# A two-layer hybrid decoder step on one core: sink as a score column, first roots in banks, other names for four banks

## The chip, the core and the metric

The kernel runs on one core of one Trainium2 chip. Time is device microseconds (us) from the start of the program to its end. Before the change the median of three runs is 2172.99 us. The engines are called PE (matrix products), ACT (elementwise functions), DVE and POOL (elementwise arithmetic) and SP (issues the large loads). PE writes to eight PSUM banks; ACT and DVE read and write them too.

## The reference, cut to what matters

Two layers, each with an FFN (feed-forward), a mixer (attention beside a gated recurrence) and a second FFN, on 512 prompt positions and 8 sequences of 8 sample positions, width 1024. Between the stages stands a root-mean-square norm with a modulation taken from a vector c.

```python
mod = (jax.nn.silu(c) @ w_ada + b_ada)
sh1, sc1, g1, sh2, sc2, g2, sh3, sc3, g3 = jnp.split(mod, N_MOD, axis=-1)
x = x + FFN_RES * g1 * swiglu(modulate(x, sh1, sc1), w1_gate, w1_up, w1_down)
h = modulate(x, sh2, sc2)              # rms_norm(x) * (1 + sc) + sh
q, k, v, xr, gr = jnp.split(h @ w_in, SPLITS, axis=-1)
...
s = s - slopes * dist
s = jnp.where(valid[:, None, None], s, NEG_INF)
sink = jnp.broadcast_to(sinks..., s.shape[:-1] + (1,))
p = jax.nn.softmax(jnp.concatenate([s, sink], axis=-1), axis=-1)[..., :-1]
...
x = x + g2 * (merged @ w_out)
x = x + FFN_RES * g3 * swiglu(modulate(x, sh3, sc3), w2_gate, w2_up, w2_down)
```

The softmax has one more column than there are keys, the learned sink of the head; its weight enters the sum and nothing else.

## The kernel before

Activations lie transposed: 1024 features as 8 blocks of 128 partitions, 576 positions in two halves of 288 columns, h=0 (64 sample positions and 224 of the prompt) and h=1. Float32 operands are split into a high and a low part: ACT writes the high part (`split` L218, a cast at L219), DVE or POOL the low part (L220). A product of one weight block with one half is three matmuls 128x288: high by high, high by low, low by high. The order on PE is the order in which the program writes matmuls and transposes (`pin` ties each to the one before); on the other engines it is set by a scheduler that follows the same program.

**The start.** `first_norm` (L383) makes the first roots: five diagonal matrices, and 12 small matmuls by ones that spread the roots over all partitions, into the tp and nrm banks; ACT copies them to SBUF (L402, `reps`). `ada_first` (L339) makes the modulation in four quarters q: 64 small matmuls of cT with weights that come by DMA into the pv bank, a copy on DVE (L349), one transpose (L209 into tp), and the bias (L354, L359). Quarter 0 stands on PE before the norm's 12 matmuls. `opened` then modulates feature blocks 2q and 2q+1 of both halves (`modulate` L544: DVE L560, L565 for the sample columns, DVE L569, ACT L580 for the high part, DVE L581 for the low part). In the first weight pair the six products of `jobs` go round by round: round q adds feature blocks 2q and 2q+1, so it needs quarter q. `E2` says before which product of a round the next quarter's matmuls and, at the second number, its transpose stand. `jobs` runs j, then h, then wi (0 gate, 1 up): the first two products of a round read h=0, the next two h=1. Of the eight weight splits of the pair, POOL makes six and DVE two.

**Openings.** Where a stage follows another, `opening` (L270) starts the next stage's first four products while the last feature block of x is still being added up. `pend` is the norm of x; `pend.add` puts a square (ACT, L131) into a bank named by `self.rest` and adds it to `acc` on DVE (L132). `PEND` and the line after the first product say at which product this stands, and with that which of the mm banks, taken in turn, the scratch gets. There are five openings (L206, `ps_mm<-hn,t`). After them `act` (L640) makes the silu of the pair; `self.modded` holds it behind the last high part of `modulate`.

**Attention.** `sample_chain` (4 a layer, one softmax each) and `prompt_chain` (8 a layer, two each) write scores into an sc bank. `soft` (L1258): DVE adds the distance term, takes the row maximum with the sink (L1263) and subtracts the sink from it (L1265); ACT takes the exponentials and their sum (L1267) and that of the sink (L1268); DVE adds (L1269), inverts (L1270) and, with ACT, scales P (L1275, L1273). PE then transposes P into tp. `keys` and `queries` (L992, L996) transpose the tokens of one block into tp, from where ACT and DVE scale them into SBUF (L1008, L1010). While these chains run, PE also has the products of the mixer (`ps_mm`), woven in by hand. Norms inside the mixer go through `tick` (L1222): `reduce` of one norm, `finish` LAG ticks later, then the next. The later ada blocks (`ada_steps`, L478) end with a DVE copy (L496) that the transposes at L500 wait for.

## Time and profile before

| | us |
|---|---|
| median of three runs | 2172.99 (2168.06 to 2173.04) |
| the profiled execution | 2171.54 |
| its span | 2169.7 |
| PE busy / DVE busy / ACT busy / POOL busy | 2099.1 / 1556.5 / 1014.7 / 778.7 |

A row of a timeline has: start in us, duration in us, engine, source line, operation, output<-inputs, shapes, count, and in brackets the engine's idle time before it with what ended that. Successive rows of an engine overlap a little, since instructions are pipelined; the step is the difference of the starts. A row of the list of waits has the engine and line that waited, what it waited for, and then: us in total, times, longest. A row of the table of windows has, for each stretch, its length, the busy time and the instruction count of each engine, the granted PE clock as a share of full speed, DMA share and GB/s. L1263 is a line of the code above.

### The profile page before, as it was taken

To read this page: it belongs to the slowest core of one execution; us is meant where nothing else is said; L and a number is where in the kernel's file an instruction comes from. 1 tells how busy PE (TensorE), PEld (TensorE's weight loads), DVE (VectorE), ACT (ScalarE), POOL (GpSimd) and SP (SyncE) were. 2 spreads that over 40 slices of the span, in tenths; PEclk is the share of its full clock that TensorE was granted. 3 is DMA by queue.
4 is the path that set the end of the run, shared out by engine and by line. 5 is a ranking of instruction groups with operands and counts; after the bars stand their busy time and mean duration, and the time that the engine had idled before them with its cause. 6 is when DMAs were issued, how large, how long until landed. Compare 5 with 4: busy or idle time off the path is not lost.

```text
span 2169.7 us, 40424 instructions
## 1 busy us (share of the span) xinstructions
PE 2099.1 (97%) x15856; PEld 1978.3 (91%) x15856; DVE 1556.5 (72%) x3701; ACT 1014.7 (47%) x2305; POOL 778.7 (36%) x671
## 2 busy tenths in 40 slices
PE   6999999999999999999999999999999999999999
PEld 6889789999879888889999999999997899999998
DVE  5766677675787876576678866776677789677665
ACT  4333434366575433333354543344566664334432
POOL 2142323344427432233245333232552474323430
PEclk8999999999999999999999999999999999999999
DMA  8844633331212265464341322232313022223221
GB/s 293 279 146 171 225 114 114 98 117 45 72 49 80 88 223 196 174 214 136 117 159 56 111 80 83 89 107 78 98 44 79 23 77 95 82 91 104 81 75 45
DMA packets 162364, 250.11 MB, mean 115 GB/s; under 512 B 7275, under 2 KB 125435, under 8 KB 154974
## 3 DMA queue, kind: packets, MB, share of 16 engines
q1 hardware_dynamic: 162018, 247.46, 34.7%
q8 instruction: 124, 2.03, 0.4%
q14 instruction: 66, 0.54, 0.1%
q10 hardware_dynamic: 156, 0.07, 0.0%
HBM read 244.62 MB, written 4.87 MB: 115 GB/s over the span
## 4 chain that ended last, share of the span: by engine, by line
PE 66%; DVE 8%; ACT 4%; issue 3%; POOL 1%; DMA 0%; ACTq 0%; POOLq 0%
PE ps_mm L843 19%; PE ps_mm L206 12%; PE ps_mm L918 8%; PE ps_sc L918 8%; PE ps_sc L843 7%; PE ps_sc L206 6%; DVE u L896 2%; ACT wh L219 2%; PE ps_pv L491 1%; PE ps_pv L206 1%; DVE wl L220 1%; ACT t L219 1%; DVE u L220 1%; PE ps_tp L209 1%; PE ps_nrm L206 1%
## 5 line engine op out<-in xcount | busy, mean ns | idle before, releaser
L849 POOL TENSOR_TENSOR P<-raw 128x512 f32<-128x512 f32 x156 | 233.1, 1507 | 724.5 <-DVE wl L220 421.4
L219 ACT CAST wh<-raw 128x512 fp32r<-128x512 f32 x498 | 298.6, 619 | 343.6 <-PE ps_mm L843 103.6
L220 DVE TENSOR_TENSOR wl<-raw,wh 128x512 fp32r<-128x512 f32 x408 | 328.6, 818 | 58.2 <-ACT wh L219 45.3
L219 ACT CAST wh<-P 128x512 fp32r<-128x512 f32 x312 | 188.0, 618 | 285.7 <-PE ps_sc L918 185.4
L220 DVE TENSOR_TENSOR wl<-P,wh 128x512 fp32r<-128x512 f32 x312 | 249.4, 814 | 83.6 <-ACT wh L219 75.2
L843 PE MATMUL ps_mm<-hn,wh 128*128 128x288 f32 x1248 | 255.6, 296 | 0.3 <-ACT t L882 0.3
L843 PE MATMUL ps_sc<-hn,wh 128*128 128x288 f32 x1248 | 254.9, 296 | 0.0
L843 PE MATMUL ps_mm<-u,wh 128*128 128x288 f32 x936 | 222.7, 299 | 5.1 <-ACT t L878 3.3
L843 PE MATMUL ps_mm<-t,wh 128*128 128x288 f32 x936 | 221.2, 297 | 0.7 <-DVE t L855 0.6
L843 PEld LDWEIGHTS ps_mm<-hn,wh 128*128 128x128 f32 x1248 | 199.8, 188 | 11.1 <-issue 6.7
L843 PEld LDWEIGHTS ps_sc<-hn,wh 128*128 128x128 f32 x1248 | 200.2, 188 | 9.2 <-issue 9.2
L843 PE MATMUL ps_mm<-hn,wl 128*128 128x288 f32 x624 | 184.0, 295 | 1.4 <-DVE wl L220 1.4
L843 PE MATMUL ps_mm<-u,wl 128*128 128x288 f32 x624 | 184.4, 296 | 0.0
L843 PE MATMUL ps_sc<-hn,wl 128*128 128x288 f32 x624 | 184.0, 295 | 0.0
L918 PE MATMUL ps_sc<-t,wh 128*128 128x288 f32 x608 | 180.7, 297 | 2.6 <-DVE ps_sc L648 1.8
L918 PE MATMUL ps_mm<-t,wh 128*128 128x288 f32 x608 | 179.5, 300 | 3.5 <-ACT t L219 2.8
L918 PE MATMUL ps_mm<-u,wh 128*128 128x288 f32 x608 | 179.8, 297 | 2.6 <-DVE u L220 2.6
L918 PE MATMUL ps_sc<-u,wh 128*128 128x288 f32 x608 | 179.9, 296 | 0.9 <-DVE u L220 0.9
L918 PE MATMUL ps_mm<-t,wl 128*128 128x288 f32 x608 | 178.9, 296 | 0.9 <-DVE wl L220 0.9
L918 PE MATMUL ps_sc<-t,wl 128*128 128x288 f32 x608 | 179.4, 295 | 0.0
L843 PEld LDWEIGHTS ps_mm<-u,wh 128*128 128x128 f32 x936 | 158.3, 188 | 18.0 <-ACT t L878 7.7
L843 PEld LDWEIGHTS ps_mm<-t,wh 128*128 128x128 f32 x936 | 158.8, 188 | 11.7 <-issue 5.4
(412 smaller groups left out, 5412.7 us busy)
## 6 DMA issues: line engine op xcount, KB each, us to landing
raw<-in_w_ada_dram SPq DMA_DIRECT2D x60, 1024.0 KB
raw<-in_w_gate_dram SPq DMA_DIRECT2D x44, 1024.0 KB
raw<-in_w_up_dram SPq DMA_DIRECT2D x44, 1024.0 KB
raw<-in_w_down_dram SPq DMA_DIRECT2D x44, 1024.0 KB
raw<-in_w_in_dram SPq DMA_DIRECT2D x14, 1024.0 KB
raw<-in_w_ada_dram SPq DMA_DIRECT2D x16, 512.0 KB
raw<-in_w_out_dram SPq DMA_DIRECT2D x4, 1024.0 KB
raw<-in_w_out_dram SPq DMA_DIRECT2D x8, 512.0 KB
```

The lines of the kernel that those rows point to most:

```text
L206: return self.pin(self.nc.tensor.matmul(*a, **k))
L209: return self.pin(self.nc.tensor.transpose(*a, **k))
L219: a = self.nc.scalar.copy(hi, src)
L220: b = (self.nc.gpsimd if pool else self.nc.vector).tensor_tensor(lo, src, hi.bitcast(F32), ALU.subtract)
L491: nc.tensor.matmul(acc[32 * j:32 * j + 32, :n], self.cT[:, k, :], raw[:, j * n:(j + 1) * n], start=(k == 0), stop=(k == KT - 1), tile_posi ...
L843: nc.tensor.matmul(ps[:, :HALF], a[x][:, k, :], b[k][y], start=start and k + n == 0, stop=k == 3 and n == 2, skip_group_check=True)
L849: nc.gpsimd.tensor_tensor(t, s[x] if x == 1 else x, s[y] if y == 2 else y, op)
L896: nc.vector.tensor_tensor(c, c, gate[i][:, hs], ALU.mult)
L918: mm(ps[:, :HALF], u[x][:, f, :], hid[f][y][:, hs], start=f + n == 0, stop=f == nf - 1 and n == 2)
```

## The change

- **Sink as a column.** P gets a column for the sink, filled by an ACT copy ahead of the scores; the exponential with its sum runs over it, and the subtraction (L1265), the sink's own exponential (L1268) and the addition (L1269) go. Each of the 40 calls of `soft` loses two small DVE instructions and one of ACT; 40 ACT copies come.
- **First roots kept in banks, gate products first.** The norm's matmuls stand ahead of quarter 0 on PE, in tp and pv, and `modulate` reads the roots there; the two ACT copies go. POOL makes all eight splits. `jobs` runs wi, j, h. `E2` is (3,4) in rounds 0 to 2.
- **Opening scratch** is named behind the second product instead of the first.
- **Silu** of the openings is held behind feature block 3 alone.
- **Queries** of blocks 3 and 4 go to the pv bank instead of tp.
- **Tick** waits one more tick between a `finish` and the next `reduce`.
- **ada_steps**' copy goes from DVE to ACT.

```diff
-E1, E2, E3 = True, ((2, 4), (0, 2), (0, 1), ()), 6
+E2 = ((3, 4), (3, 4), (3, 4), ())
...
-                if pend and h == 0 and (b, k) == (0, 0):
+                if pend and h == 0 and (b, k) == (1, 0):
                     self.rest(pend.add(KT - 1, self.done.pop((KT - 1, 1))))
...
-            acc = self.ps("pv")
+            acc = self.start[1][:, HALF:]
...
-            tp = self.ps("tp")
+            tp = self.start[0][:, HALF:]
...
-        reps = [self.ps(tag) for tag in ("tp", "nrm")]
+        reps = self.start = [self.ps(tag) for tag in ("tp", "pv")]
...
-            nc.vector.tensor_copy(ev[:, :n], acc[:, :n])
+            nc.scalar.copy(ev[:, :n], acc[:, :n])
...
+            if k == 3:
+                self.modded = r
...
-                    jobs = [(j, h, wi) for j in range(2) for h in range(2) for wi in range(2)]
+                    jobs = [(j, h, wi) for wi in range(2) for j in range(2) for h in range(2)]
...
-            tp = self.ps("tp")
+            tp = self.ps("tp" if t < 3 else "pv")
...
-        elif self.queue and self.queue[0][1] <= self.now:
+        elif self.now > self.idle and self.queue and self.queue[0][1] <= self.now:
...
-        nc.vector.tensor_tensor(es, nm, sinks, ALU.subtract)
         for i, p in enumerate(pts):
             nc.scalar.activation(p, p, AF.Exp, bias=nm[:, i:i + 1], scale=-1.0, accum_out=dn[:, i:i + 1])
-        nc.scalar.activation(es, es, AF.Exp)
-        nc.vector.tensor_tensor(dn, dn, es, ALU.add)
...
+        for kv in range(NKV):
+            nc.scalar.copy(pt[kv][:, :, nk * W], self.skp[:, l, gp, 2 * kv:2 * kv + 2])
```

PE at the start, before the change, from the transpose of quarter 1 on (each product is six such rows, of which one stands; hn is the modulated x, wh and wl weights, pT the copied quarter):

```order
L209 MATMUL ps_tp_420<-ident,pT_406 128x128 [waits DVE_49]
L206 MATMUL ps_mm_337<-hn_301,wh_315 128x288
...
L206 MATMUL ps_nrm_338<-hn_301,wh_327 128x288
...
L206 MATMUL ps_pv_458<-t_205,cT 32x128 [waits DMAHW4_49,PE_49]
...
L206 MATMUL ps_mm_333<-hn_301,wh_309 128x288 [waits Activation_49]
...
L206 MATMUL ps_sc_334<-hn_301,wh_321 128x288
```

And with the change:

```order
L207 MATMUL ps_nrm_330<-hn_295,wh_309 128x288
...
L210 MATMUL ps_tp_225<-ident,pT_405 128x128 [waits DVE_49]
L207 MATMUL ps_sc_331<-hn_295,wh_315 128x288
...
L207 MATMUL ps_mm_332<-hn_295,wh_315 128x288
...
L207 MATMUL ps_mm_327<-hn_295,wh_303 128x288 [waits Activation_49]
...
L207 MATMUL ps_mm_328<-hn_295,wh_303 128x288 [waits Activation_49]
```

Between the transpose and the next round's first product there are now two products, and no ada matmuls (ps_pv); the second product of a round reads h=1 where it read h=0.

DVE in the first sample chains of layer 0, before, after the root steps (L533 to L535) of a keys block; the P, sm and ps_sc are those of `soft`:

```order
L1008 TENSOR_SCALAR u_6309<-ps_tp_6484,qg 128x128 [waits Activation_49]
...
L1130 TENSOR_TENSOR u_6287<-u_6287,ps_mm_6417 128x512 [waits DVE_49]
L1269 TENSOR_TENSOR sm_6502<-sm_6502,sm_6501 128x1 [waits Activation_49]
L1263 ISA P_6546,sm_6547<-ps_sc_6540,nds,sks,sel 128x192 [waits PE_49]
...
L1270 RECIPROCAL sm_6502<-sm_6502 128x1 [waits DVE_49]
L1265 TENSOR_TENSOR sm_6548<-sm_6547,sks 128x1 [waits DVE_49]
L1275 TENSOR_SCALAR P_6499<-P_6499,sm_6502 128x192 [waits DVE_49]
```

And with the change:

```order
L1268 RECIPROCAL sm_6490<-sm_6490 128x1 [waits Activation_49]
L532 SCALAR_TENSOR_TENSOR ps_mm_6405<-tiny_6438,ps_mm_6405 128x8 [waits DVE_49]
L1273 TENSOR_SCALAR P_6487<-P_6487,sm_6490 128x192 [waits DVE_49]
L1129 TENSOR_TENSOR u_6275<-u_6275,ps_mm_6405 128x512 [waits DVE_49]
L1007 TENSOR_SCALAR u_6297<-ps_tp_6472,qg 128x128 [waits Activation_49]
L1264 ISA P_6531,sm_6533<-ps_sc_6525,nds,sks,sel 128x192 [waits PE_49]
...
L1268 RECIPROCAL sm_6534<-sm_6534 128x1 [waits Activation_49]
L1273 TENSOR_SCALAR P_6531<-P_6531,sm_6534 128x192 [waits DVE_49]
```

The inversion and the scaling of the first P now stand ahead of L1129 (L1130 before), and so does their wait for ACT's exponential; the second query copy of the block (L1007, L1008 before) has moved from ahead of these rows to behind them.

PE at the queries of block 3 in layer 0, before:

```order
L206 MATMUL ps_mm_7109<-hn_5430,wl_6681 128x288
L209 MATMUL ps_tp_7153<-ident,u_6379 128x128 [waits PE_49]
L209 MATMUL ps_tp_7153<-ident,u_6379 128x128 x3
L206 MATMUL ps_sc_7162<-u_6305,u_6308 128x256 [waits DVE_49]
...
L209 MATMUL ps_tp_7209<-ident,P_7045 128x128 [waits DVE_49]
```

And with the change:

```order
L207 MATMUL ps_mm_7067<-hn_5418,wl_6660 128x288
L210 MATMUL ps_pv_7111<-ident,u_6367 128x128 [waits PE_49,Activation_49]
L210 MATMUL ps_pv_7111<-ident,u_6367 128x128 x3
L207 MATMUL ps_sc_7120<-u_6293,u_6296 128x256 [waits DVE_49]
...
L210 MATMUL ps_tp_7161<-ident,P_7009 128x128 [waits DVE_49]
```

The transposes go to pv and wait for ACT as well; the transposes of P that follow are the same.

## Rows read from the trace of the kernel before

**Rows 1.** The page's busy times (us, share of the span, instructions)

```profile
PE 2099.1 (97%) x15856; PEld 1978.3 (91%) x15856; DVE 1556.5 (72%) x3701; ACT 1014.7 (47%) x2305; POOL 778.7 (36%) x671
```

**Rows 2.** The list of waits, engine PE, whole span

```profile
PE ps_mm L206 <- DVE acc L132: 6.9, 5, 1.4
PE ps_pv L206 <- DMA raw<-in_w_ada_dram: 6.4, 2, 4.0
PE ps_mm L206 <- ACT hn L580: 5.2, 1, 5.2
PE ps_tp L209 <- DVE P L1275: 4.4, 2, 2.2
PE ps_tp L209 <- DVE u L1008: 3.5, 2, 1.8
PE ps_tp L500 <- DVE pT L496: 2.3, 1, 2.3
PE ps_nrm L206 <- DVE ps_mm L593: 2.1, 2, 1.1
PE ps_sc L206 <- DVE ps_sc L648: 1.6, 3, 0.5
```

**Rows 3.** Timeline of the start, PE and DVE

```profile
24.08 1.78 PE L206 MATMUL ps_tp<-diag,ones 64*128 64x64 f32 x6
26.99 0.42 PE L209 MATMUL ps_tp<-ident,pT 128*128 128x128 f32 x1
28.10 0.69 DVE L220 TENSOR_TENSOR wl<-raw,wh 128x512 fp32r<-128x512 f32 x1
28.91 1.75 DVE L220 TENSOR_TENSOR wl<-raw,wh 128x512 fp32r<-128x512 f32 x1
32.60 0.61 PE L206 MATMUL ps_mm<-hn,wh 128*128 128x288 f32 x1 [5.18 <-ACT hn L580]
```

**Rows 4.** Table of windows, a stretch of the start and one after a wait

```profile
34.00:36.00 2.00, 2.00 (x9) 1.82 (x8) 1.37 (x4) 0.56 (x2) 0.00 (x0) 0.50 1.09 348
36.00:38.00 2.00, 2.00 (x66) 1.71 (x65) 0.00 (x0) 0.00 (x0) 0.00 (x0) 0.99 1.09 349
941.00:944.00 3.00, 3.00 (x15) 3.00 (x14) 1.55 (x5) 0.27 (x1) 0.00 (x0) 0.50 0.62 180
```

**Rows 5.** Timeline of the second round, PE and DVE

```profile
39.68 0.27 PE L209 MATMUL ps_tp<-ident,pT 128*128 128x128 f32 x1
43.35 0.53 PE L206 MATMUL ps_mm<-hn,wh 128*128 128x288 f32 x2
44.26 0.51 DVE L581 SCALAR_TENSOR_TENSOR hn<-nt,mod,hn 128x288 fp32r<-128x288 f32 x1
```

**Rows 6.** Timeline of two openings, PE and POOL

```profile
697.06 1.46 POOL L578 TENSOR_TENSOR hn<-nt,hn 128x224 fp32r<-128x224 f32 x2
1550.33 1.86 PE L206 MATMUL ps_mm<-hn,t 128*128 128x288 f32 x12 [1.35 <-DVE acc L132]
1550.76 0.67 POOL L578 TENSOR_TENSOR hn<-nt,hn 128x224 fp32r<-128x224 f32 x1
```

**Rows 7.** Timeline, ACT at the later ada copy

```profile
937.80 0.61 ACT L219 CAST wh<-raw 128x512 fp32r<-128x512 f32 x1
```

**Rows 8.** Timeline of a sample chain, PE, POOL and DVE

```profile
1626.78 0.33 PE L209 MATMUL ps_tp<-ident,u 128*128 128x128 f32 x1
1628.90 2.49 POOL L220 TENSOR_TENSOR wl<-raw,wh 128x512 fp32r<-128x512 f32 x2 [2.52 <-ACT wh L219]
1629.02 1.17 DVE L1265 TENSOR_TENSOR sm<-sm,sks 128x1 f32<-128x1 f32 x1
1630.11 1.40 DVE L1275 TENSOR_SCALAR P<-P,sm 128x192 f32<-128x192 f32 x1
1631.65 0.41 PE L209 MATMUL ps_tp<-ident,P 128*128 128x128 f32 x2 [2.20 <-DVE P L1275]
```

**Rows 9.** Timeline, ACT at the queries of block 3

```profile
1670.47 0.50 ACT L1273 ACTIVATE P<-P,sm 128x256 f32<-128x256 f32 x1
```

More of the change, by code (lines that the diff above doesn't have):

```diff
@@ L53 @@
 SLOT = 608
+SINK = 2 * 128 + 1
 STEPS = (1, 4)
@@ L164, in __init__ @@
         self.done = {}
-        self.now, self.cur, self.queue, self.ended = 0, None, [], []
+        self.now, self.idle, self.cur, self.queue, self.ended = 0, -1, None, [], []
     BUFS = {"t": 14, "u": 12, "P": 4, "pT": 3, "raw": 4, "wh": 4, "wl": 4, "hn": 4, "sq": 2, "acc": 2, "nt": 3, "mod": 2,
@@ L398, in first_norm @@
                             start=True, stop=True)
-        self.reps = []
-        for ps in reps:
-            self.reps.append(self.t("sq", [P, HALF]))
-            nc.scalar.copy(self.reps[-1], ps[:, :HALF])
     def params(self):
@@ L1449, in run @@
         first = self.ada_first(0, loads)
-        if E1:
-            next(first)
         self.first_norm()
-        if not E1:
-            next(first)
+        next(first)
         next(first)
@@ L1460, in opened @@
                 for h in range(2):
-                    self.modulate(hn, h, self.mods[0], 0, self.reps[h], 2, range(2 * q, 2 * q + 2))
+                    self.modulate(hn, h, self.mods[0], 0, self.start[h], 2, range(2 * q, 2 * q + 2))
                 yield q
```

45 lines of the change are left out of this document (24 added, 21 removed).

## The prediction

> **What bounds the kernel now.** I read the busy times first: PE is busy for 2099.1 of 2169.7 us [rows 1], so only about 70 us of the span are PE waiting, and the change leaves PE the same matmuls and transposes. Other engines matter only where PE waits for them. The second view is therefore the list of PE's waits, in which the reader is to look for the lines that the change touches [rows 2]: the openings' accumulation (L132, five waits, 6.9 us), the first modulated block (L580, 5.2), P of the softmax (L1275, 4.4 in two), the query copies (L1008, 3.5 in two), the ada copy (L496, 2.3), a norm's reduce (L593, 2.1 in two) and the silu's product (L648, 1.6 in three). Together 26.0 us; no edit can give more than that by waits alone. The third view are the timelines around each, to see what is late next. The table of windows adds the PE clock: at 34 to 36 us it is at half (1.2 of 2.4 GHz), 9 matmuls in 2.00 us; from 36 on it is full; at 941 to 944, behind the wait for the ada copy, it is at half once more [rows 4]. So a wait can cost more than its length: 3.0 us at half give back about 1.5.
>
> The sum is made against the profiled execution's own 2171.54 us (1.84 around the span). The median of the three runs is 1.45 above it, inside their spread.
>
> **Start.** PE idles 5.18 us ahead of the first product at 32.60 [rows 3]. Two things leave that path. The norm's 12 matmuls and the transpose behind them run from 24.08 on; the transpose comes at 26.99 [rows 3]. Ahead of quarter 0 they would run inside a wait for DMA of which PE has 6.4 us [rows 2], so the transpose moves up by up to 2.9 us. The two weight splits on DVE, 0.69 and 1.75 [rows 3], go to POOL: up to 2.3 by their steps (the second ends in a step of 1.67). The ACT copies of the roots were beside this. At most that is 5.2. Against it, POOL now makes four splits of the second weight beside the modulation, where it made two, and a DVE instruction beside POOL can be late by about one split: 1.75 against 0.69 is such a case. I take 4.5, with 3.3 to 5.8 as bounds.
>
> The new order takes some of it back. From the transpose at 39.68 to the end of the last low part of h=1 (44.26 and 0.51) are 5.1 us [rows 5]. Before, the next round's first product came 3.67 us behind the transpose, at 43.35 [rows 5], with the ada matmuls in between, and h=1 was needed only by the third product; no wait shows. Now two products stand between, and the second product of the round reads h=1. Twelve matmuls run in 1.86 us with the tail of the last one, 1.6 by their step [rows 6]. So PE has 1.6 us for the two products, 0.8 for the round's first and about 0.7 of the second: 3.1 of the 5.1. It waits 2.0 in each of three rounds: 6.0 us in all, 4.5 to 6.6 as bounds, by how early DVE is.
>
> The clock rose some 3.5 us after products began [rows 3, 4]. If it rises as late after an earlier start, nothing changes; if it rises at 36 as now, 4.5 us more run at half and 2.3 are lost. I take 1.0, with 0 and 4.0 (2.3, and one fall to half as at 941) as bounds. Start in all: 4.5 - 6.0 - 1.0 = 2.5 us lost, bounds 7.3 lost and 1.3 gained.
>
> **Openings.** The second product waited for a bank that Square and the addition of block 6 still read. It gets the free bank; the scratch, which is needed later, takes the late one. Next late are the low parts that POOL makes: in the mixer's opening one ends at 1551.43 (1550.76 and 0.67), while PE began again at 1550.33; in the second FFN's two end at about 697.8 [rows 6], where PE waited until 698. I take 1.05 for each of the two mixer openings, 0.75 for each of two in front of the second FFN and 1.55 for the fifth: 5.2 us, 2.5 to 6.9 as bounds.
>
> **Silu.** Held behind block 3 instead of block 7, the silu leaves ACT ahead of eight high parts. The three waits for L648 are 1.6 us [rows 2]; all goes, 0 to 1.6.
>
> **Ada copy.** PE waits 2.3 us for DVE's copy [rows 2]. On ACT it stands behind the cast at 937.80 that ends at 938.4 [rows 7], so it is done about 1.1 earlier than now. The fall to half behind it [rows 4] may go as well. I take 1.5, 0 to 4.0. The other eight copies show no wait.
>
> **Sink.** Off the path each call loses small work that DVE and ACT had room for, and 40 small ACT copies are hidden as long as ACT has them ahead of the scores. What counts are the two waits for P of the first sample chain, 4.4 us [rows 2]: L1265 takes 1.17 us for one column, then L1275 takes 1.40, both beside POOL [rows 8]. Without L1265 this P is ready before PE asks for it. But DVE's inversion, which waits for ACT's exponential behind its table load, now heads the queue in front of L1129 and of the second query copy, which frees the tp bank that the keys transpose uses at 1626.78, today without a wait [rows 8]. By the length of that queue I put the bank about 2.0 us later and the new wait at 1.8 in each layer. 4.4 - 3.6 = 0.8 us, with -1.2 and 4.4 as bounds.
>
> **Queries.** The two waits of P for the tp bank, 3.5 us [rows 2], go, for the queries no longer hold it. Next is P itself, whose last scaling on ACT starts at 1670.47 [rows 9], 2.7 us before PE gets there. The pv bank is read by ACT just before the queries; PE may wait a little there. I take 3.3, 1 to 3.5.
>
> **Tick.** One tick later the reduce has its accumulation: the 2.1 us for L593 [rows 2] go, 0 to 2.1.
>
> Rest: 5.2 + 1.6 + 1.5 + 0.8 + 3.3 + 2.1 = 14.5 us (low ends 2.3, high ends 22.5). With the start 14.5 - 2.5 = 12.0, and 2171.54 - 12.0 = 2159.5; I say **2160**.
>
> **The rivals.**
>
> *The queues give it back (0.25).* A freed wait only uncovers the next late instruction, as POOL's low parts do in the openings. For: four of the terms have a known next one. Against: most of the waits touched are for one instruction alone. With the low ends to a third of the terms, 2 to 6 us less the 2.5 of the start: about **2170**, no change.
>
> *A small DVE instruction is blocked by POOL (0.12).* L1265, on one column, began at 1629.02, just after POOL's first of two splits (2.49 us together from 1628.90), and ended when that split did; L1275 likewise with the second [rows 8]. If what blocks is POOL's running split and not DVE's queue, then taking L1265 away only lets the next DVE instruction block: P is ready one split (1.25) earlier, not two, so 2.5 of the 4.4; and at the start the three small DVE instructions ahead of the first product can each meet one of POOL's four splits, 2 us more. 0.8 becomes -1.1, the start -4.5: **2163.5**. The Trainium skill, page "SBUF — State Buffer", section "SBUF: two separate sides", says that DVE and GpSimd share a port pair as "an exclusive lock, not a bandwidth split", held for the whole instruction. By that rule this rival holds, and the rows agree with it for L1265.
>
> *The start is better than worked out (0.12).* If ACT and DVE make h=1 sooner than in the second round of before, the waits are 1.5 and the clock rises early: start 1.3 gained, rest as above or higher: **2154**.
>
> *Slower (0.09).* The three waits of the start let the clock fall to half and it stays there through rounds 1 to 3. Their 108 matmuls then step by 0.22 instead of 0.14 [rows 4, 6], 8.6 us at the least and up to 12; the start loses about 13. It decides as soon as the rest brings under 6 us, by the same uncovered waits: with 4, 2171.5 + 13 - 4 = **2180**. For: the clock was at half behind a wait of 2.3 us [rows 2, 4]. Against: PE works through most of each round, and between the three waits it has several us of products.
>
> **How the numbers follow.** My forecast has 0.42. A measurement of this kernel can tell about 0.3%, 6.5 us, from no change. Faster holds the forecast, the blocked DVE and the better start: 0.66. Same holds the queues: 0.25. Slower: 0.09. All low ends together give 2171.5 - 2.3 + 7.3 = 2176.5, all high ends 2171.5 - 22.5 - 1.3 = 2147.7; neither is likely as a whole. The range 2149 to 2174 takes in all but the slower case and a little at the fast end.
>
> **What would show it.** In the changed kernel's list of waits the rows for L132 in the openings, L496, L593 and the query copies should be gone or under 0.5 us each. The first product should stand at 27 to 29 us, and PE should show three waits of about 2 us for high or low parts ahead of the second products of rounds 1 to 3. A wait of a keys transpose for a query copy would show the sink's new queue. The forecast is wrong if those first-round waits are absent (then better), if the clock row stays at half beyond 40 us (then worse), or if the openings wait on POOL as long as they waited on DVE.

## The result: 0.6% slower, and the profile after

| | before | after |
|---|---|---|
| median, us | 2168.07 (2167.85 to 2173.04) | 2183.91 (2180.20 to 2192.03) |
| profiled execution, us | 2171.54 (span 2169.7) | 2182.75 (span 2181.0) |
| ratio after : before | | 1.0063, 95% interval 1.0047 to 1.0079 |

The forecast was 2160, faster; the time came out 13.7 us above the kernel before by the ratio (10 to 17; 15.8 by the medians) and outside the range. The list of waits of the changed kernel, engine PE, whole span, the first rows (columns as in [rows 2]):

```profile
PE ps_tp L210 <- ACT pT L1306: 5.8, 6, 1.7
PE ps_tp L210 <- ACT t L307: 5.3, 1, 5.3
PE ps_mm L207 <- ACT hn L577: 4.6, 1, 4.6
PE ps_tp L207 <- DVE diag L394: 4.4, 1, 4.4
PE ps_tp L497 <- ACT pT L493: 4.4, 2, 3.3
PE ps_mm L842 <- ACT t L877: 3.8, 4, 1.3
PE ps_tp L210 <- DVE u L1007: 3.4, 2, 1.7
PE ps_pv L207 <- ACT pT L1341: 3.0, 2, 1.5
PE ps_mm L917 <- ACT t L220: 2.6, 3, 1.3
PE ps_mm L917 <- DVE u L221: 2.6, 6, 0.7
PE ps_mm L842 <- ACT hn L220: 2.2, 3, 1.0
PE ps_mm L207 <- POOL hn L575: 2.1, 4, 0.7
...
PE ps_mm L842 <- POOL hn L221: 0.9, 3, 0.5
```

Beside [rows 2] the waits that the change aimed at are gone: the openings' accumulation (L132), P of the softmax (L1275), the reduce (L593), the silu's product (L648). What came in their place is on the list: ACT's copies of transposed P (L1306, L1341), the ada copy on ACT (L493), POOL's low parts in the openings (L575), and, ahead of the products of the pairs (L842), casts (hn L220) and low parts that POOL makes (L221), three times each. Behind an opening the next pair of gate and up weight blocks is multiplied by Strassen's scheme, seven products of sums of blocks in place of eight; `sums` makes the sums of the modulated x, and ACT, DVE and POOL split them. The list is not long enough for a loss: its rows come to 64 us, and to 63 before. So I took the start of the n-th of PE's 15856 matmuls in one trace less that of the n-th in the other, and read where this difference grows:

| stretch, us of before | growth, us |
|---|---|
| 0 to 274, start and first FFN up to its third group | +4.7 (it had been +9.4 at 105) |
| 274 to 512 | -1.3 |
| 512 to 684, layer 0's mixer | +4.9 |
| 684 to 824, second FFN's opening and first Strassen pair | +2.9 |
| 824 to 1165, with the ada copy at 937 and the next opening | -4.6 |
| 1165 to 1235, first FFN of layer 1, silu and first pair | +3.5 |
| 1235 to 1779, layer 1's mixer and openings | -2.5 |
| 1779 to 1850, second FFN, silu and first pair | +3.7 |
| sum with the end | +11.3 |

The three first pairs behind openings, of which the prediction says nothing, hold 11 us (3.7, 3.5 and 3.8 read from 4 to 17 us behind each opening's wait to the end of the pair); the start holds 5. Four of the five openings and the ada copy are in the minus rows. In layer 0's mixer 3.0 of the 4.9 come at the clock: behind the new wait for L1341 (1.5 us at 595) it is granted at 0.62 and 0.70; behind the same wait of 1.5 us in layer 1 (at 1664) it stays at 1.00 (windows of the changed kernel, [rows 4] has the columns):

```profile
595.00:600.00 5.00, 4.56 (x27) 3.77 (x28) 2.42 (x14) 2.70 (x13) 0.00 (x0) 0.62 0.32 89
600.00:605.00 5.00, 5.00 (x30) 5.00 (x29) 1.60 (x8) 2.59 (x11) 0.00 (x0) 0.70 0.62 120
```

The table sets one execution against one. The last section shows two stretches, and the part on the start a third, in which the one profile of the kernel before is not like other executions; a row of the table is an edit's doing only where the runs below show it.

### The profile page after: what moved, and what is told of

It is laid out like the page before. It is cut to its first block, busy times and chain, and to the rows that moved or that the text cites. A ratio compares the mean times of both kernels' runs of the same rounds, so it can differ in the third digit from the quotient of the medians.

```text
span 2181.0 us, 40338 instructions
## 1 busy us (share of the span) xinstructions
PE 2107.8 (97%) x15856; PEld 1980.4 (91%) x15856; DVE 1546.2 (71%) x3610; ACT 1020.2 (47%) x2312; POOL 780.3 (36%) x673
## 5 line engine op out<-in xcount | busy, mean ns | idle before, releaser
L848 POOL TENSOR_TENSOR P<-raw 128x512 f32<-128x512 f32 x156 | 228.3, 1475 | 724.6 <-DVE wl L221 385.7
L220 ACT CAST wh<-raw 128x512 fp32r<-128x512 f32 x498 | 298.6, 619 | 332.4 <-PE ps_mm L842 93.9
L221 DVE TENSOR_TENSOR wl<-raw,wh 128x512 fp32r<-128x512 f32 x406 | 336.6, 842 | 62.2 <-ACT wh L220 49.6
L220 ACT CAST wh<-P 128x512 fp32r<-128x512 f32 x312 | 188.4, 619 | 292.3 <-PE ps_sc L917 184.5
L221 DVE TENSOR_TENSOR wl<-P,wh 128x512 fp32r<-128x512 f32 x312 | 247.3, 806 | 87.2 <-ACT wh L220 78.7
L842 PE MATMUL ps_mm<-hn,wh 128*128 128x288 f32 x1248 | 256.1, 296 | 3.1 <-ACT hn L220 2.2
L842 PE MATMUL ps_sc<-hn,wh 128*128 128x288 f32 x1248 | 255.0, 296 | 1.7 <-ACT wh L220 1.7
L842 PE MATMUL ps_mm<-u,wh 128*128 128x288 f32 x936 | 221.5, 298 | 7.1 <-ACT t L877 3.8
L842 PE MATMUL ps_mm<-t,wh 128*128 128x288 f32 x936 | 220.7, 297 | 2.2 <-DVE t L854 1.9
L842 PEld LDWEIGHTS ps_mm<-hn,wh 128*128 128x128 f32 x1248 | 199.9, 188 | 14.0 <-issue 5.9
L842 PEld LDWEIGHTS ps_sc<-hn,wh 128*128 128x128 f32 x1248 | 199.9, 188 | 13.3 <-issue 10.9
L842 PE MATMUL ps_mm<-hn,wl 128*128 128x288 f32 x624 | 184.2, 295 | 2.1 <-DVE wl L221 1.8
L842 PE MATMUL ps_mm<-u,wl 128*128 128x288 f32 x624 | 184.5, 296 | 0.0
L842 PE MATMUL ps_sc<-hn,wl 128*128 128x288 f32 x624 | 183.7, 294 | 0.0
L842 PEld LDWEIGHTS ps_mm<-u,wh 128*128 128x128 f32 x936 | 157.8, 188 | 19.3 <-ACT t L877 8.6
L842 PEld LDWEIGHTS ps_mm<-t,wh 128*128 128x128 f32 x936 | 158.2, 188 | 12.6 <-DVE t L854 4.0
```

Source lines behind the costliest of these rows:

```text
L220: a = self.nc.scalar.copy(hi, src)
L221: b = (self.nc.gpsimd if pool else self.nc.vector).tensor_tensor(lo, src, hi.bitcast(F32), ALU.subtract)
L842: nc.tensor.matmul(ps[:, :HALF], a[x][:, k, :], b[k][y], start=start and k + n == 0, stop=k == 3 and n == 2, skip_group_check=True)
L848: nc.gpsimd.tensor_tensor(t, s[x] if x == 1 else x, s[y] if y == 2 else y, op)
```

## The experiments

All ratios are of runs beside the kernel before on the same chip. Seven kernels have one part of the change alone (x18 is the kernel of x4 once more):

| run | part alone | ratio, 95% interval |
|---|---|---|
| x1 | silu | 1.0045, 1.0030 to 1.0060 |
| x2 | opening scratch | 1.0011, 1.0002 to 1.0021 |
| x3 | start | 1.0050, 1.0035 to 1.0065 |
| x4, x18 | ada copy, twice | 0.9986, 0.9976 to 0.9996; 0.9992, 0.9983 to 1.0001 |
| x6 | sink | 1.0017, 1.0006 to 1.0028 |
| x7 | queries | 1.0031, 1.0016 to 1.0047 |
| x8 | tick | 0.9996, 0.9984 to 1.0009 |

Singly they sum to 1.36% (with x4), together they cost 0.63%. Silu and scratch spoil the same pairs, and sink and queries help each other, by the traces; no run has such two alone.

### Silu and scratch: the first pair pays (x1, x2)

```diff
-                self.modded = nc.scalar.copy(hk, t)
+                r = nc.scalar.copy(hk, t)
...
+            if k == 3:
+                self.modded = r
```

> The kernel before with one edit, the silu of the openings held behind feature block 3. Theory A (the edit lets the scheduler put the seven products of the first pair behind an opening in another order on PE, at three places, and there the products that read the POOL-made sums now come too early): three new losses of 3.4 to 4.0 us in those pairs, the three waits for L648 gone (about 2 us), in all 8 to 10 us slower than before. Theory B (the losses in those pairs come from the other bank of the opening's scratch): no loss there, 1.6 to 2 us faster.

Measured: 2181.29 beside 2171.98. From the middle of the opening to the end of the pair the n-th matmul falls back by 2.9, 3.1 and 3.1 us (layer 0's second FFN, both of layer 1), the silu's gain of 0.8 included. So the pair loses more than the silu gives: theory A by the time.

```diff
-                if pend and h == 0 and (b, k) == (0, 0):
+                if pend and h == 0 and (b, k) == (1, 0):
```

> The kernel before with one edit, the openings' scratch named behind the second product. Theory A with a second source (this edit too moves the three first pairs on PE): openings 5 us shorter, the pairs 10 to 12 us longer, in all 5 to 7 us slower. Theory A where only the silu's order costs: 5 us faster. Theory B: the pairs lose as in the changed kernel, 5 to 7 us slower.

Measured: 2173.62 beside 2171.98. The five openings gain 0.92, 0.77, 1.55, 0.92 and 0.76 us, 4.9 in all, where the prediction had 5.2. From 4 to 17 us behind the opening's wait to the end of the three pairs, 3.0, 1.6 and 2.1 go back, 6.8 in all, and part of it in the opening itself: PE's wait for the silu's product (L648) is 3.7 where it was 1.6 [rows 2]. So the openings are as forecast, and the pairs lose less than the 10 to 12 of theory A.

Why does a silu that comes earlier hurt a pair 15 us later? VectorE's queue in the kernel before, timeline (start us, us, line, op, tiles), and in x1:

```profile
725.78 0.46 DVE L763 TENSOR_TENSOR ps_pv<-ps_pv,hn 128x288 f32<-128x288 f32 x1
726.14 0.46 DVE L763 TENSOR_TENSOR ps_tp<-ps_tp,hn 128x288 f32<-128x288 f32 x1
...
726.87 0.23 DVE L593 TENSOR_TENSOR ps_mm<-ps_mm,mod 128x64 f32<-128x64 f32 x1
```

```profile
724.49 0.22 DVE L595 TENSOR_TENSOR ps_mm<-ps_mm,mod 128x64 f32<-128x64 f32 x1
...
732.93 0.45 DVE L765 TENSOR_TENSOR ps_pv<-hn,ps_nrm 128x288 f32<-128x288 f32 x1
...
736.90 0.46 DVE L765 TENSOR_TENSOR ps_tp<-ps_tp,hn 128x288 f32<-128x288 f32 x1
```

Before, the Strassen block sums up to the third block's (`sums`, L763) end at 726.6, and then the first residual update (`update`, L593) begins. In x1 the updates begin at 724.49, the third block's sums are still undone, and the updates after that wait for PE's down products one by one; the sums come at 732.93 and 736.90. ACT and POOL follow, in x1:

```profile
737.44 0.43 ACT L219 CAST hn<-acc 128x288 fp32r<-128x288 f32 x1
737.95 0.81 POOL L220 TENSOR_TENSOR hn<-acc,hn 128x288 fp32r<-128x288 f32 x1 [14.06 <-ACT hn L219]
744.41 0.43 ACT L219 CAST hn<-acc 128x288 fp32r<-128x288 f32 x1 [2.58 <-POOL P L851]
```

POOL waits 14 us, the last block's cast is at 744.41 (741.35 before), and PE waits in the pair, 736 to 756 us, where the kernel before has no wait:

```profile
PE ps_mm L845 <- ACT hn L219: 0.9, 1, 0.9
PE ps_sc L845 <- ACT wh L219: 0.6, 1, 0.6
PE ps_mm L845 <- POOL hn L220: 0.3, 1, 0.3
```

Neither edit touches `sums`, `update` or the pair. The scheduler that writes each engine's queue ordered them anew. That holds for PE too. Against what is said further up of PE's order, `pin` ties only the matmuls of `mm` and `tr`; the pair's products, many down products and the adaLN steps are left to the scheduler. In the kernel before PE weaves the products into ps_sc and ps_mm from 741 to 750 us, in ten stretches; in x1 it takes them almost one after the other, in four from 739 to 752. That is the mechanism of x1's theory A, and it is not told apart here from DVE's order.

### Which queue (x5, x9, x10)

My first reading was ACT's queue: its cast of the third block stood behind weight casts that wait 8.27 us for PE.

```diff
-        b = self.split(hi, lo, src)[1]
+        a, b = self.split(hi, lo, src)
+        self.np += 1
+        if self.np > 4:
+            self.order(self.t3, a)
```

> The kernel before with the silu edit (x1) and one order edge added: ScalarE may cast the fifth and later weight parts of a pair only behind the cast of the third block of t3, which is where the kernel before had it. Theory A, order: in x1 that cast stood behind weight casts that wait for TensorE's last down product (8.27 us), so GpSimd's last sum of t3 came at 740.4 in place of 727.3 and the pair waited. With the edge the silu waits stay away (-0.7 at each of three openings) and each of the three first pairs loses 0 to 1 us in place of 3 to 5: 2166 to 2171 beside a kernel before of 2168 to 2172, ratio 0.997 to 1.001. Rival B, handed on: the pairs lose because TensorE now reaches them earlier than the sums can be ready, whatever the order: losses of 3 to 5 us each stay, about 2179 to 2181, ratio about 1.0045 as in x1.

Measured: 2182.91 beside 2169.56, ratio 1.0064 (1.0048 to 1.0080). The edge put that cast ahead, at 738.89, later than in x1, since it now waited for a DVE sum, and the pairs lost 4.1, 4.3 and 3.6. The theory fell for ACT, and the time is on rival B's side. That the pairs lose whatever stands first doesn't follow, as the next run shows.

```diff
                     self.opening(wo, xs, ("mm", "mm", "sc", "sc"), pend, done)
+                    for _ in range(3):
+                        bs = next(sums)
```

> The kernel before with the silu edit (x1), and three of the four steps of the Strassen block sums called right behind the opening, ahead of the first group's down products, so that VectorE's queue has the sums of the third block ahead of the residual updates again. Theory A, VectorE's order: in x1 and x5 the rest of these sums stood behind the updates, which wait for TensorE's down products until 737, so ScalarE's and GpSimd's third block followed at 737 to 740, whatever their own order (x5). With the sums ahead the first pairs lose 0 to 1 us each, the silu gain of 0.7 at each opening stays: 2165 to 2171 beside a kernel before of 2168 to 2172, ratio 0.997 to 1.001. Rival B, handed on: the pairs lose 3 to 5 us each whatever stands first, ratio 1.0045 to 1.006 as in x1 and x5. Rival C: the sums now hold the updates back and TensorE's down products wait for their banks, 1 to 2 us at each of three places, ratio 1.001 to 1.003.

Measured: 2175.84 beside 2170.61, ratio 1.0024 (1.0013 to 1.0035): about half of x1's loss went (1.0045, with an interval that overlaps). Opening and pair come to 3.6, 0.6 and -0.1 us (2.9, 3.1, 3.1 in x1). In layer 1 the loss is gone, in layer 0 it is not. The late updates hold PE's down products now at all three places, 1.8, 1.5 and 1.8 us, rival C, which also had the time; in layer 1 the pair gives that back. The waits of x9, engine PE, 726 to 760 us (layer 0):

```profile
PE ps_mm L922 <- DVE xT L600: 1.0, 2, 0.8
PE ps_sc L922 <- DVE xT L600: 0.8, 1, 0.8
```

DVE is nearly full in this stretch whatever the order: busy for 18.0 of the 20 us from 726 to 746 in x9, 18.1 in x1 and 18.6 in the kernel before, so sums and updates compete. In layer 0 the clock also fell to half for 3.4 us at 735 (0.91 over these 20 us), 1.7 of the 3.6. What else keeps layer 0's loss is open. So is which queue did it: x9 changes PE's order in the pair along with DVE's.

```diff
+            if k == 3:
+                self.modded = r
...
+                if pend and h == 0 and (b, k) == (1, 0):
...
+            nc.scalar.copy(ev[:, :n], acc[:, :n])
...
+                        bs = next(sums)
```

> The kernel before with the scratch, silu and ada copy edits and the three steps of block sums called right behind the opening. Theory A (x9's): openings -5.3 as in x2, silu -2, the copy at 937 -2.9, first pairs 0 to +1 each: -7 to -10, 2158 to 2163, ratio 0.9955 to 0.997. Rival B: the pairs' losses of 3 to 4 us each stay: 0 to +2, ratio 1.000 to 1.001.

Measured: 2171.87 beside 2170.61, ratio 1.0004 (0.9994 to 1.0013). The time is rival B's. By the trace it lies between the theories: the pairs cost 4.5, 0.8 and 2.0 us, and the openings' gain, 4.9, pays for most of that.

### The start (x3, x11 to x14, x17)

```diff
-E1, E2, E3 = True, ((2, 4), (0, 2), (0, 1), ()), 6
+E2 = ((3, 4), (3, 4), (3, 4), ())
...
-        reps = [self.ps(tag) for tag in ("tp", "nrm")]
+        reps = self.start = [self.ps(tag) for tag in ("tp", "pv")]
...
-                    jobs = [(j, h, wi) for j in range(2) for h in range(2) for wi in range(2)]
+                    jobs = [(j, h, wi) for wi in range(2) for j in range(2) for h in range(2)]
```

> The kernel before with one edit, the new start (first roots in banks, gate products first, all eight splits on POOL). If what the changed kernel shows up to 100 us belongs to the start alone: first product near 29.3 us, three round waits of about 2 us, 4 to 5 us slower. If the wait at the first ada transposes (3.9 us near 105) also comes from the start's order: 8 to 9 us slower.

Measured: 2181.82 beside 2171.98. PE's n-th matmul is 5.9 us behind at 65 us of before and 13.5 at 105, behind the first down product; by 256 4.7 of that are back, most of it in waits that the kernel before has there and x3 has not or has shorter, for DVE's low parts of weights and for adaLN weights, in the kernel before:

```profile
PE ps_pv L491 <- DMA raw<-in_w_ada_dram: 2.6, 2, 1.5
```

The changed kernel itself at the start, timeline, 23.2 to 29.6 us:

```profile
23.39 4.98 POOL L221 TENSOR_TENSOR wl<-raw,wh 128x512 fp32r<-128x512 f32 x4 [2.34 <-ACT wh L220]
...
24.38 0.33 PE L210 MATMUL ps_tp<-ident,pT 128*128 128x128 f32 x1 [0.45 <-DVE pT L350]
...
24.85 0.28 DVE L557 TENSOR_TENSOR nt<-xT,ps_tp 128x128 f32<-128x128 f32 x1
25.05 0.87 DVE L360 TENSOR_SCALAR mod<-mod 128x18 f32<-128x18 f32 x1
25.95 1.30 DVE L562 TENSOR_TENSOR nt<-nt,mod 128x128 f32<-128x128 f32 x1
...
29.29 0.61 PE L207 MATMUL ps_mm<-hn,wh 128*128 128x288 f32 x1 [4.59 <-ACT hn L577]
```

Beside [rows 3] the transpose moved up by 2.6 us and the first product by 3.3, to 29.29 from 32.60. But ten other traces have the start of the kernel before (x1, x2, x4 to x10, x18). In them the transpose stands at 24.5 to 26.1 (median 24.9) and the first product at 28.9 to 31.7 (median 29.3); here is x1:

```profile
24.51 0.28 PE L209 MATMUL ps_tp<-ident,pT 128*128 128x128 f32 x1
28.91 0.61 PE L206 MATMUL ps_mm<-hn,wh 128*128 128x288 f32 x1 [4.12 <-ACT hn L580]
```

So 32.60 belongs to one execution: PE ran the norm's matmuls at half clock in it (six in 1.78 us [rows 3], in 1.05 in x1), and its wait was 5.18 where nine of the ten have 4.1. In the eight traces with the roots in banks the transpose has a median of 24.4 and the first product one of 29.1. The edit moved the transpose by half a microsecond, and a gain of the first product can't be told. What stands between transpose and product is the rival of the blocked DVE: 18 columns took 0.87 us and a 128x128 addition of two tiles of the scratch (nt, mod) 1.30, where these rows took 0.18 and 0.29 in the kernel before (at 27.68 and 27.89) ahead of POOL's splits. The 128x128 form that reads ps_tp, a bank, for its second operand took 0.28, and all of it lies inside POOL's four splits. The Trainium skill's rule of an exclusive lock ("SBUF — State Buffer", section "SBUF: two separate sides") names among the blocked the DVE forms with two SBUF inputs; the 1.30 and the 0.28 agree with it. Then the rounds, windows of the changed kernel over 18 matmuls, three products into ps_mm, the last of one round and the first two of the next, at rounds 1 and 2 (length; busy us and count of PE, PEld, DVE, ACT, POOL; clock; DMA):

```profile
37.66:42.17 4.51, 3.69 (x20) 2.54 (x19) 3.93 (x11) 2.12 (x5) 0.00 (x0) 1.00 1.08 386
46.78:51.56 4.78, 3.45 (x20) 2.54 (x19) 4.78 (x12) 2.12 (x5) 1.56 (x2) 1.00 0.12 27
```

18 matmuls at 0.13 are 2.4 us; they take 4.5 and 4.8 at full clock. That is the wait of about 2 us in each round that the prediction forecast. From 40 to 65 us of before PE falls back by 7.0 us in each of five traces with both halves of the edit (x3, x14, x16, x17 and the changed kernel).

x11 and x12 take the edit apart: banks and reading order on the one side, product order, the places of the adaLN steps and the POOL splits on the other.

```diff
-        reps = [self.ps(tag) for tag in ("tp", "nrm")]
+        reps = self.start = [self.ps(tag) for tag in ("tp", "pv")]
...
-            nc.scalar.copy(self.reps[-1], ps[:, :HALF])
```

> The kernel before with the half of the start edit that keeps the first roots in their banks (no copies to the scratch, the first transposes behind the norm), the products in the old order. Theory A: the banks bring the first product some 3 us earlier (29.3 in after, 32.6 before), and the loss of x3 (13 us by 117, 10 at the end) belongs to the product order: -1 to -4 here, ratio 0.998 to 0.9995. Rival B: the loss belongs to the banks, since VectorE's small work behind them stands beside GpSimd's splits and the adaLN's steps come later: +4 to +10, ratio 1.002 to 1.005.

```diff
-                    wt = [[self.wsplit(r[:, :, j * P:(j + 1) * P], (KT, P), (j, wi) != (0, 1)) for j in range(2)] for wi, r in enumerate(raws[0])]
+                    wt = [[self.wsplit(r[:, :, j * P:(j + 1) * P], (KT, P), True) for j in range(2)] for wi, r in enumerate(raws[0])]
...
+                    jobs = [(j, h, wi) for wi in range(2) for j in range(2) for h in range(2)]
```

> The kernel before with the other half of the start edit: the four gate products ahead of the four up products, all four first weight splits on GpSimd and the adaLN steps at the other places, the roots copied to the scratch as before. Theory A: this half carries the loss, the rounds' waits of about 2 us each and ScalarE's queue behind the casts of GpSimd's sums at 104 to 113: +7 to +12 in all, ratio 1.003 to 1.0055. Rival B: 0 to +3, since the waits only come with the earlier first product, ratio 1.000 to 1.0015.

Measured: x11 2174.45 beside 2170.61, ratio 1.0017 (1.0007 to 1.0026); x12 2188.42, ratio 1.0081 (1.0066 to 1.0096). x12 agrees with its theory and goes further. Its first product stands at 32.93 behind a wait of 6.26, about 2 us longer than in the old start: four splits on POOL in place of two, the rival of the blocked DVE once more. The rounds then lose 10.4 us by 65, 7.0 as in x3 and 3.4 by the clock: from 56 to 62 us it is at half, the mechanism of the prediction's slower rival, in a kernel that has only half of the edit:

```profile
56.00:62.00 6.00, 5.55 (x72) 4.91 (x72) 0.39 (x1) 0.00 (x0) 2.29 (x6) 0.50 0.01 3
```

x11 gave neither result. Its start is 0.6 us ahead at 65 us, no more than the ten traces with the old start (0.1 to 2.5); then it loses 7.4 us at one place, the first down product, as the timeline shows:

```profile
104.48 0.43 ACT L219 CAST hn<-acc 128x288 fp32r<-128x288 f32 x1 [2.92 <-POOL acc L759]
...
107.83 0.43 ACT L219 CAST hn<-acc 128x288 fp32r<-128x288 f32 x1 [2.62 <-POOL acc L759]
108.17 4.26 ACT L219 CAST wh<-raw 128x512 fp32r<-128x512 f32 x8
...
108.83 0.61 PE L914 MATMUL ps_mm<-t,wh 128*128 128x288 f32 x1 [7.33 <-ACT wh L219]
```

All eight casts of the down weights stand behind four casts of sums that POOL still makes; in the kernel before, weight casts at 93.83 and 94.68 stood ahead of them. One order edge puts the first four back:

```diff
-            self.split(*b12[k], a, T3POOL)
+            r = self.split(*b12[k], a, T3POOL)[0]
+            if not banks and not k:
+                self.order(self.early, r)
```

> x11 with one order edge: the four casts of the first down weights (raw issued at 85.2 in both kernels) stand ahead of ScalarE's cast of the first block of t3, as three of them did in the kernel before. Theory A, ScalarE's order: in x11 all eight weight casts came behind four casts that wait for GpSimd's sums (2.1, 2.9 and 2.6 us), so the first down product waited 7.3 us at 101.5. With the edge this wait goes and the third of a promille that the banks bring stays: -4 to +1 us, ratio 0.998 to 1.0005. Rival B: the wait comes from the weights' arrival or from GpSimd's sums, and another wait of 5 to 7 us stands in its place within 20 us: ratio 1.001 to 1.002 as in x11 (1.0017).

Measured: 2169.80 beside 2170.48, ratio 0.9998 (0.9986 to 1.0009). Theory A: the wait is gone, 2.6 us of another (for residual updates at 127) came instead.

```diff
+                    if l == gi == s0 == 0 and c0 + c == nw:
+                        self.early = self.cast
```

(the same edge, on x3; `cast` is the last weight cast so far)

> x3 (the whole start edit) with the same order edge. Theory A: of its loss of 13 us by 117 the 4 to 5 us at 104 to 113 go, of which the later waits for adaLN weights had taken up a part: +5 to +8 in all, ratio 1.0025 to 1.004 beside 1.005 in x3; the rest is the rounds' waits up to 65 us. Rival B: nothing goes, ratio 1.0045 to 1.0065.

Measured: 2179.26 beside 2170.48, ratio 1.0043 (1.0030 to 1.0057), between the theories. Here the first down product still waits 3.4 us, and no longer for the queue: ACT's first weight cast is at 110.79, behind a wait of 3.88 for the weights' own load. The queue that issues the loads, x14:

```profile
65.90 36.39 SPq L485 DMA_DIRECT2D raw<-in_w_ada_dram  x7
103.70 1.24 SPq L716 DMA_DIRECT2D raw<-in_w_down_dram  x2
```

The first down weights are issued at 103.70, in the kernel before at 85.80. Seven adaLN loads wait ahead for buffers, and the adaLN products that free these run from 93.9 on, where they ran at 75.4, 83.8 and 92.2 before. The changed kernel is the same there: its first down weights are issued at 103.31. The DMA engines have a share of 0.01 from 80 to 90, where the kernel before has 0.88.

```diff
+                        if l == gi == s0 == 0 and n < 3:
+                            self.behind = self.adamm
```

(the next product's first matmul is ordered behind that one)

> x14 with one more order: in the second pair of layer 0 each product's first matmul stands behind the adaLN products of the product before, as in the kernel before, where they ran at 75.4, 83.8 and 92.2; in x14 none ran between 70.1 and 93.9, the queue of loads stood on seven adaLN loads from 65.9 to 102.3, the DMA engines were idle (0.01 of 80 to 90), and the first down weights were issued at 103.7 (85.8 before). Theory A, queue: with the adaLN products earlier their buffers come free earlier, the down weights are issued before 98, the first down product's wait of 3.4 falls below 1.5: ratio 1.002 to 1.0035 beside 1.0043 in x14. Rival B: TensorE now waits for the adaLN weights instead, ratio 1.004 to 1.006.

Measured: 2178.79 beside 2170.50, ratio 1.0037 (1.0028 to 1.0047). The queue, x17:

```profile
66.19 27.01 SPq L488 DMA_DIRECT2D raw<-in_w_ada_dram  x7
95.53 4.73 SPq L721 DMA_DIRECT2D raw<-in_w_down_dram  x2
```

The down weights are issued 8 us earlier and the wait of 3.4 is gone from PE's list: theory A for the place. The time lies at the edge of what it gave, for 2.6 us of a wait for residual updates came at 131, as in x13, and x14 and x17 can't be told apart by their intervals. What is left of the start is 4.8 us by 69 us against the one profile of before, the rounds.

### Attention (x6, x7, x8)

```diff
-        nc.vector.tensor_tensor(es, nm, sinks, ALU.subtract)
...
+            nc.scalar.copy(pt[kv][:, :, nk * W], self.skp[:, l, gp, 2 * kv:2 * kv + 2])
```

> The kernel before with the sink as a column of the scores alone. The prediction's step: -0.8 in all (2.2 us off each layer's sample chain, 1.8 back at the keys). Theory A, from the trace of after: per layer the key transposes wait 1.7 more, the wait for P goes (-2.35), and the product with the values gets a new wait of 1.3 to 1.5, so +0.5 to +1 per layer: +1 to +2 in all, ratio 1.0005 to 1.001. Rival B: the chain gain is kept whole and the keys' wait belongs to another edit: -4 in all, ratio 0.998.

Measured: 2173.82 beside 2169.56, ratio 1.0017. Its waits, engine PE, 555 to 645 us (layer 0):

```profile
PE ps_tp L210 <- ACT pT L1308: 2.6, 3, 1.4
PE ps_tp L210 <- DVE u L1009: 2.3, 2, 1.7
PE ps_pv L207 <- ACT pT L1343: 1.5, 1, 1.5
```

The wait of 2.2 for P is gone, as forecast, and the keys transpose waits 1.7 for a query copy, forecast at 1.8. Not forecast: 1.5 for ACT's copy of the transposed P, and 2.6 for copies that cost 0.9 before. ACT got the column copies ahead of the scores, and its copies of P come later. Theory A by sign; the size is above what it gave, though the interval holds it.

```diff
-            tp = self.ps("tp")
+            tp = self.ps("tp" if t < 3 else "pv")
```

> The kernel before with the last query tile's transposes in the values' bank alone. The prediction's step: -3.3 in all, from a wait of 1.92 us per layer that goes and some of which comes back. Theory A, from the trace of after: -1.9 per layer, then waits of 1.25 and 0.7 that come 10 to 20 us later: 0 per layer, -0.5 to +0.5 in all, ratio 0.9995 to 1.0005. Rival B: those later waits belong to the sink or the tick, and the edit alone keeps -3 to -4, ratio 0.998 to 0.9985.

Measured: 2177.18 beside 2169.56, ratio 1.0031, outside both. The wait of 1.9 goes, and the queries' own transposes wait for the values' bank, in layer 0 at 626.24 (2.08 us), since ACT empties it behind softmax scalings and two weight casts:

```profile
624.74 1.12 ACT L219 CAST wh<-raw 128x512 fp32r<-128x512 f32 x2
625.77 0.42 ACT L1318 COPY u<-ps_pv 128x128 f32<-128x128 f32 x2
626.24 0.66 PE L209 MATMUL ps_pv<-ident,u 128*128 128x128 f32 x4 [2.08 <-ACT u L1318]
```

Waits for copies of transposed P stand ahead of it (0.5) and behind it (0.9 and 1.9), and behind the last one the clock falls (windows of x7):

```profile
635.00:645.00 10.00, 8.11 (x51) 5.88 (x51) 5.49 (x26) 4.96 (x18) 0.00 (x0) 0.87 0.01 2
645.00:655.00 10.00, 10.00 (x53) 8.85 (x53) 5.78 (x26) 2.52 (x7) 2.32 (x3) 0.62 0.00 0
```

0.87 and 0.62 in place of 1.00 are 5 us of full clock; in layer 1 two stretches at 0.83 are 3.4. With the sink's edit beside it, in the changed kernel, the same wait is 1.3 us in two. There ACT no longer has the sinks' own exponentials; that this is the reason is argued, not shown.

```diff
-        elif self.queue and self.queue[0][1] <= self.now:
+        elif self.now > self.idle and self.queue and self.queue[0][1] <= self.now:
```

> The kernel before with the pause of one tick between two norms' chains alone. The prediction's step: -2.1 in all. Theory A, from the trace of after: -1.1 at layer 0 and about the same at layer 1: -2.2 in all, ratio 0.999. Rival B: the pause puts the next norm's reduction late, and its readers wait: 0 to +2, ratio 1.000 to 1.001.

Measured: 2169.26 beside 2169.56, ratio 0.9996. The wait for L593 is gone in both layers, and 0.7 us a layer are left of it by the n-th matmul; the time doesn't tell whether they stay gained.

### The ada copy, and what is left together (x4, x18, x15, x16)

```diff
-            nc.vector.tensor_copy(ev[:, :n], acc[:, :n])
+            nc.scalar.copy(ev[:, :n], acc[:, :n])
```

> The kernel before with one edit, the copy of the later ada blocks on ACT. If the copy's place in ACT's queue behind the casts of the POOL-made sums is what PE waits for near 105 us: a new wait of 3 to 4 us there, 2.8 us gained near 937, in all 0 to 1.5 us slower. If that wait needs the new start: 2.5 to 3 us faster.

> The ada copy edit alone once more, with more rounds (x4 gave 0.9986 with an interval of 0.9976 to 0.9996): it is the one edit of the change that was faster by itself. Theory A: the wait of 2.3 us at 937 is gone and nothing takes its place, ratio 0.998 to 0.9995. Rival B: the gain lay in undisturbed stretches of x4 alone, ratio 0.9995 to 1.0005.

x18 has the copy alone, whatever its label says. Measured: 2168.71 beside 2171.98, and 2169.67 beside 2170.50. The wait at 937 is 2.3 us in [rows 2], but 1.4 in x6, which has the copy on DVE too. In all thirteen traces of other kernels with DVE's copy it is 1.4 to 2.2 (median 1.5), in the six with ACT's 1.0 to 1.6 (median 1.1). The half clock behind it [rows 4] is missing in all but two of the thirteen, too. So most of the 2.3 lay in the one profiled execution, and the edit takes about 0.4 off. The gain is 0 to 5 us by the intervals, not settled more closely.

```diff
+            nc.scalar.copy(ev[:, :n], acc[:, :n])
...
+        reps = self.start = [self.ps(tag) for tag in ("tp", "pv")]
...
+                self.order(self.early, r)
```

> The ada copy edit, the banks half of the start edit and the cast edge together. Theory A: the ada copy's -3 (x4) and the banks' -1 to -2 add up: -3 to -6, ratio 0.997 to 0.9985. Rival B: ScalarE's copies of the adaLN products stand behind its casts at 104 as in after (a wait of 3.3), and the gain is lost: ratio 0.9995 to 1.001.

Measured: 2169.71 beside 2170.48, ratio 0.9995 (0.9987 to 1.0004), no gain that can be told. That is rival B's time, but not its wait: at 104 none shows, and 2.6 us for residual updates stand at 128, as in x13.

```diff
+                        bs = next(sums)
...
+                self.order(self.early, r)
```

(both on the changed kernel)

> The kernel after with both order changes, three steps of block sums ahead of the first group's down products (x9) and the down weights' casts ahead of t3's (x13). Theory A: the two order shifts are about half of what after loses: 2 promille from the sums (x9 against x1), 1 to 2 from the casts: ratio 1.002 to 1.0035 against 1.0063 of after. Rival B: the edits' own new waits in attention and in the start's rounds carry the loss: ratio 1.005 to 1.0065.

Measured: 2182.30 beside 2170.48, ratio 1.0063 (1.0044 to 1.0081), as without: rival B by the time. In the trace the pairs of layer 1 improve (2.1 and 0.8 us for 3.5 and 3.7) and the end is 2.3 us earlier, but the cast edge meets the late load as in x14 (12.8 us behind at 105 of before, against 9.4), so theory A held for a part only. None of the kernels beats the one before beyond its interval but x4, and x18, the same kernel, does not.

## Why the prediction was wrong

1. **Silu (+1.6) and openings (+5.2)** failed as the step that costed an edit by its own wait alone. Both waits went as forecast (4.9 in the openings, 0.8 per silu in x1). The step took it that nothing else moves. But the queues are written by a scheduler, and each edit turned DVE's sums and residual updates around in three pairs, and PE's products in them: 11 us in the changed kernel, 9 in x1, 7 in x2. That these places cost more than the waits gave is shown by x1 and x2. For x1, x9 shows that the order of the queues, with the same edit, makes up about half of the time; whether it is DVE's order or PE's is open, and that the same holds for the scratch edit is argued from the same rows and from x10, not shown alone.
2. **Start (-2.5).** Right: the rounds' waits, a little over 2 us each, 7.0 for 6.0 and above the bound of 6.6. Failed: the first product's gain, 4.5. The two profiles show 3.3, but beside the ten other traces with the old start it is 0.2 by the medians, under the stated lower bound of 3.3. The late transpose and the wait of 5.18 that it was worked out from were those of one execution, and the two splits taken off DVE came back as DVE's wait beside POOL, the rival with 0.12 (about 2 us in x12). The clock rose at 33 in the changed kernel, 3.7 us behind the first product, so its 1.0 was not lost there; in x3 it rose at 36.6, and it was. Missed: what the new order does behind 65 us. In the start edit alone 4.5 us were lost ahead of the first down product (3.7 there, 0.8 at the ada copy before it), whose weights came in late because adaLN products moved some 18 us on and held the load buffers (x14, x17); in x11, where the load is in time, because of ACT's queue (x13). In the changed kernel the wait at this place shows at ACT's ada copy (3.3 us). "The queues give it back" was the rival nearest to this, but its price stopped at no change.
3. **Ada copy (+1.5).** "The other eight copies show no wait" held for the kernel before only. In x4 they show none at 104; in the changed kernel PE waits 3.3 us for one there, behind the casts of POOL's sums. And the 2.3 us were for the most part of one execution: the copy's place on ACT is worth about 0.4.
4. **Sink (+0.8).** Right about what goes (2.2 a layer) and about the keys (1.7 for 1.8). Missed: ACT's later copies, 3 us a layer. Measured alone: +3.7 us.
5. **Queries (+3.3).** "PE may wait a little there" was the term: 2.1 us a layer for the values' bank in x7, up to 1.9 for copies behind it, and the clock at half. Alone it costs 6.7 us; in the changed kernel, with the sink, the waits about cancel.
6. **Tick (+2.1).** The wait went; the time moved by less than can be told.

The sum took its gains from one trace, and two of them, 4.5 and 1.5, were for the most part that trace's own. One more reading was off without an effect: of the two low parts in the second FFN's opening [rows 6] the first ends at 697.8, the second at 698.5. The chance of the slower case failed with the terms: 0.09 for one mechanism at the start, where most terms could turn negative by the same other one, a queue put in another order.

## What to carry to other kernels

Where a scheduler writes the queues, an edit's price is not its own wait: look ahead through the next 20 us of every engine's queue for a pair of jobs that could change places (here sums against updates on DVE, weight casts against casts of POOL's sums on ACT, adaLN products on PE against the loads behind them), and compare the order there before trusting a gain of a few us. Take a gain from a trace only where a second execution shows the wait too. Measure the parts of a bundle alone: two of these seven were at or below the time of before, and the whole was not their sum. A bank or buffer that looks free is priced by the queue of the engine that empties it.

## What the runs showed of the hardware beyond that

The blocking beside POOL goes with where a DVE form's second operand lies: 1.30 us with both in the scratch, 0.28 with one in a bank, at the same size, in one row of each kind.

And two profiled executions differ without any edit. In x4, x5, x9, x14 and x18 the matmuls between 558 and 611 us fall behind the kernel before by 4.1 us, in a stretch that these edits don't touch; x7 and x8 do the same there. It is the clock. In each of the seven it is granted at half for 10.2 us, from between 566 and 577 on, behind the wait of 2.2 us for P; behind the same wait the kernel before keeps full clock. Windows of before and of x4:

```profile
570.00:575.00 5.00, 4.33 (x41) 3.48 (x41) 3.41 (x18) 3.15 (x10) 2.49 (x2) 1.00 0.59 204
570.00:575.00 5.00, 4.33 (x26) 3.03 (x27) 1.91 (x13) 1.70 (x5) 2.49 (x2) 0.50 0.44 168
```

In x1, x2, x3, x11, x13 and x15 it does not fall there either. So the clock's part of a wait is not fixed by the wait, and the fall in the changed kernel at 595 may be such a one. A gain of a few us in one profile is therefore not yet a gain.
